# Gate and up projections of a SwiGLU block in seven half-width products per pair of blocks, weight sums on VectorE

## The chip, the cores and the metric

One core of a Trainium2 chip. The metric is the device time of one execution in microseconds (us); the time before is the median of three runs. TensorE (PE) multiplies, PEld is its weight load, VectorE (DVE) and ScalarE (ACT) do elementwise work, GpSimd (POOL) does a little, SyncE (SP) starts the transfers. A "release" below is the moment at which an instruction's input or its buffer becomes available.

## The reference, cut to what matters

Two layers; each is a mixer (a state-space half and a retention half), cross-attention to a memory, and a SwiGLU block. Only the last is changed:

```python
def swiglu(h, w_gate, w_up, w_down):
    return (jax.nn.silu(h @ w_gate) * (h @ w_up)) @ w_down
# h: 512 tokens x 1024, w_gate and w_up: 1024 x 2816, w_down: 2816 x 1024, all f32
x = x + swiglu(rms_norm(x, norm_ffn[l]), w_gate[l], w_up[l], w_down[l])
```

## The kernel before, in words

Everything is transposed: activations lie as 128 channels by 512 tokens, so the hidden width 2816 is 22 blocks f of 128, and the inner width 1024 is 8 blocks kt. Each f32 operand is cut into two parts of the type fp32r, a rounded copy (hi, made by ACT) and the rest (lo, a subtraction on DVE); a product of two such operands is three matmuls, hi*hi, hi*lo and lo*hi (`mm3`, lines 469 to 473). The norm's gain goes into the activations before the product (`Norm.tile`, lines 599 to 608), its 1/rms into the result afterwards (`nrm.bc`).

Weights come in chunks of 128x1024 (512 KB). `prep_chunk` (451 to 459) loads one into a slot of the kind `raw`, and makes hi and lo in two slots of the kind `w`; `chunk` asks for them four chunks ahead in program order. There are 3 raw slots and 6 w slots, that is three chunks of hi and lo. Other tiles of 128x512 come from 66 slots of the kind `u`, and PSUM from 8 banks.

`ffn` (1337 to 1367) runs over parts of the hidden width (`FPARTS`, line 32: three parts in layer 0, four in layer 1). In a part, for each f, `proj` forms gate and up, each as 24 matmuls of 512 columns into one bank; then DVE multiplies both by `nrm.bc`, ACT takes the silu, DVE multiplies the two, and `split` cuts the result into hi and lo. After the part's last f the down projection adds the part's share to x for each of 8 output blocks. In layer 0, four pieces of the next layer's state-space tables (`s5_spill`) are hung behind f = 5, 9, 13 and 17. The last part of layer 1 goes through `last_down`, in two halves of 256 columns.

The program order is not the order on the engines. All operations are recorded, and a planner (`Program.due` and `schedule`, lines 247 to 379) lays them out: it prices each (`price`), gives each a due time from its users, and in a simulated time gives each free engine the most urgent operation whose inputs and slots are ready, TensorE included, which may so take matmuls of a later product first. A slot is handed out when its first operation is placed, and comes back 250 ns after its last reader. `KEEP` is a number of u slots held back from work that is due late.

All instructions are issued through one line of `emit` (387; memsets 385), so the profile gives that line for nearly everything: tiles tell the groups apart. In the names of the profile, `u_nfh` and `u_nfl` are the hi and lo of the SwiGLU's input, `u_gs` and `u_us` gate and up, `u_acth` and `u_actl` the product's parts, `u_xoh` and `u_xol` the input of the cross-attention's output projection (`co`), which runs just before; `u_mh` and `u_ml` are the memory's parts, whose key projection multiplies 256 columns (the memory has 256 rows).

Of the kernel before, what the change touches and what calls it, by code (L numbers as in the profile page):

```python
# [10 lines left out]
F32 = mybir.dt.float32  # L11
F32R = mybir.dt.float32r
I32 = mybir.dt.int32
AF = mybir.ActivationFunctionType
# [4 lines left out]
P = 128  # L19
L = 2  # L20
D = 1024
KT = D // P
SEQ = 512
# [7 lines left out]

FPARTS = (((0, 8), (8, 15), (15, 22)), ((0, 7), (7, 13), (13, 19), (19, 22)))
HALF = SEQ // 2


# [9 lines left out]

KINDS = {"u": 66, "s": 40, "raw": 3, "w": 6, "ps": 8}
LOOKAHEAD = 4
# [9 lines left out]
TABLE, REUSE, COLD, WINDOW = 15000, 250, 7000, 30000  # L57
KEEP, FRONT = {"u": 38}, 30000

# [9 lines left out]
def chunk_order():  # L69

    o = []
    for l in range(L):
        o += [("u", l, m) for m in range(4)]
        o += [("v", l, m) for m in range(4)]
        count = {"q": 1, "k": 1, "g": 1, "ck": KT, "glu": 2, "cv": 8}
        for step in PLAN[l].split():
            key = {"Q": "q", "K": "k", "G": "g", "M": "ck", "L": "glu", "V": "cv"}.get(step[0])
            if key:
                m = int(step[1:] or 0)
                o += [(key, l, m + i) for i in range(count[key])]  # L80
        o += [("out", l, m) for m in range(KT)]
        o += [("cq", l, m) for m in range(KT)]
        o += [("co", l, m) for m in range(KT)]
        for a, b in FPARTS[l]:
            for f in range(a, b):
                o += [("gate", l, f), ("up", l, f)]
            o += [("down", l, f) for f in range(a, b)]
    return o


# [5 lines left out]
class Buf:  # L96
    __slots__ = ("kind", "real", "wr", "rd", "left", "end", "n", "s", "dt")

# [96 lines left out]
class Program:  # L195
    def __init__(self, slots):
        self.ops, self.slots = [], slots
        self.cap = CAP

    def buf(self, kind, s="", dt=None):  # L200
        b = Buf(kind, None, s)
        b.dt = dt
        return Ref(b, (), self.slots[kind][0] if dt is None else self.forms[dt])
# [4 lines left out]
    def add(self, eng, fn, k):  # L208
        o = Op()
# [4 lines left out]
        if fn == "dma_start":  # L214
            o.dur = 60 if eng == "SP" else 1000
            n = 4
            for d in k["out"].ap.shape:
                n *= d
            o.bytes = n
        else:  # L220
            o.dur = price(eng, fn, k)
# [47 lines left out]
    def schedule(self):  # L269
# [7 lines left out]
        self.due()  # L277
        order, left = [], sorted(self.ops, key=lambda o: -o.prio)
        for o in self.ops:
# [4 lines left out]
        def fits(o, low):  # L284
            need = {}
            for b in o.bufs:
                if b.kind and b.real is None:
                    need[b.kind] = need.get(b.kind, 0) + 1
            for k, n in need.items():
                keep = KEEP.get(k, 0) * min(1.0, (o.prio - low) / FRONT)  # L290
                if sum(1 for f, _ in free[k] if f <= t) < n + keep:
                    return False
            return True

        while len(order) < len(self.ops):
            while left and left[-1].end is not None:
                left.pop()
            low = left[-1].prio
            moved = False
            for e in engs:  # L300
# [41 lines left out]
                for b in o.bufs:  # L342
                    if b.kind and b.real is None:
                        f = min(free[b.kind])
                        free[b.kind].remove(f)
                        b.n = f[1]
                        b.real = self.slots[b.kind][b.n] if b.kind != "u" else 0
# [26 lines left out]
            if not nxt:  # L374
                raise RuntimeError(f"no order found: {len(order)} of {len(self.ops)}, next "
                                   f"{left[-1].eng} {left[-1].fn} "
                                   f"{ {k: len(v) for k, v in free.items()} }")
# [22 lines left out]
def trunk(ctx, tc, io):  # L400
# [33 lines left out]
    def gen(s, dt=F32):  # L434
        return prog.buf("u", s, dt)
# [9 lines left out]


    order = chunk_order()
    ready = {}
    state = {"prep": 0, "use": 0}

    def prep_chunk():
        i = state["prep"]
        state["prep"] += 1
        raw = prog.buf("raw")
        Q.dma_start(out=raw, in_=io["w"][i])
        hi, lo = prog.buf("w"), prog.buf("w")
        S.activation(out=hi, in_=raw, func=AF.Copy)
        V.tensor_tensor(out=lo, in0=raw, in1=hi.bitcast(F32), op=sub)
        ready[i] = (hi, lo)

    def chunk(*key):
        i = state["use"]
        state["use"] += 1
        assert order[i] == key, (order[i], key)
        while state["prep"] < min(len(order), i + 1 + LOOKAHEAD):
            prep_chunk()
        return ready.pop(i)

    def mm3(ps, a, b, start, stop):
# [121 lines left out]
    class Norm:  # L591


        def __init__(self, s, gcol, n=SEQ):
            self.s, self.gcol, self.n = s, gcol, n
            self.parts = [None] * KT
            self.acc = None

        def tile(self, i, x, stat=True):
            g = vec[:, self.gcol + i:self.gcol + i + 1]  # L600
            n = self.n
            hi, lo = gen(self.s + "h", F32R), gen(self.s + "l", F32R)
# [733 lines left out]

    def ffn(l, nrm, nxt, extra):
        for fa, fb in FPARTS[l]:
            acts = []
            for f in range(fa, fb):  # L1340
                pg = proj("gate", l, f, nrm)
                if f == 0:
                    nrm.root(True)
                pu = proj("up", l, f, nrm)
                gs, us = gen("gs"), gen("us")
# [5 lines left out]
                if f in extra:  # L1351
                    extra[f]()
            if nxt is None and fb == NFF:
# [142 lines left out]
    for l in range(L):  # L1496
        n_cross = Norm("nc", V_CROSS + l * KT)
        kv = mixer(l, nrm, n_cross, start if l == 0 else lambda: None)
        n_ffn = Norm("nf", V_FFN + l * KT)
        cross(l, n_cross, kv, n_ffn)  # L1500
# [17 lines left out]
def layout(inp):  # L1518
# [11 lines left out]
            "gate": f("w_gate"), "up": f("w_up")}  # L1530
    order = chunk_order()
    w = np.empty((len(order), P, D), np.float32)
    for n, (key, l, m) in enumerate(order):
# [21 lines left out]
    a["w"] = w  # L1555
    cols = lambda k: f(k).reshape(-1, P).T
    a["vec"] = c(np.concatenate(
# [46 lines left out]
```

## Time and profile before

| what | value |
|---|---|
| median of 3 runs | 1525.04 us (1524.87 to 1525.72) |
| the profiled execution | 1526.83 us, of which the span is 1525.1 us |
| mean granted clock of TensorE | 0.990 of 2.4 GHz |
| PE busy | 1499.2 us, 98% |
| DVE busy | 946.9 us, 62% |
| ACT busy | 655.0 us, 43% |
| gate and up of layer 1's second part | 1263.9 to 1329.7 us |
| its down projection | 1329.7 to 1362.7 us |

The shares are means over stages that differ. An instruction's duration on DVE and ACT is longer than the distance at which the next one can start, so costs are read as distances between starts in stretches without a gap, for matmuls too.

### The profile page before, as it was taken

The page shows a single profiled execution, that of the slowest core. Times are in us where ns is not written, and L with a number is a line of the kernel's source. Part 1 is how long each engine was busy: PE and PEld are TensorE (multiplying, and loading weights), DVE is VectorE, ACT ScalarE, POOL GpSimd, SP SyncE. Part 2 cuts the span into 40 slices and gives each one's busy share as a digit, 9 for nine tenths or more (in the row PEclk, how much of TensorE's full clock was granted, in tenths as well). Part 3 has the DMA queues.
Part 4 walks back from the last instruction along what each step waited for, and adds up shares of the span by engine and source line. Part 5 has one row for each costly group of instructions (what it writes and reads, how often), then busy time and mean ns, then how long its engine had stood idle before and what let it go on. Part 6 is the DMA issues. An engine that isn't in the chain of part 4 may idle for free.

```text
span 1525.1 us, 18872 instructions
## 1 busy us (share of the span) xinstructions
PE 1499.2 (98%) x7176; PEld 1241.0 (81%) x7176; DVE 946.9 (62%) x1602; ACT 655.0 (43%) x1050; POOL 90.3 (6%) x192
## 2 busy tenths in 40 slices
PE   8799999999999999999999999999999999999997
PEld 7688888888888888888888879788888888888887
DVE  7899986665674366454554889657656434434445
ACT  5577655444443244243335455544344322323224
POOL 4630000000011010000000000000000000000001
PEclk9899999999999999999999999999999999999998
DMA  6323444321334343344245554433123333333331
GB/s 208 104 85 111 135 120 141 97 70 56 97 114 130 97 140 123 116 125 119 93 132 173 158 165 128 128 104 97 56 70 97 97 97 97 97 97 95 93 94 65
DMA packets 66140, 168.53 MB, mean 111 GB/s; under 512 B 11137, under 2 KB 22785, under 8 KB 66049
## 3 DMA queue, kind: packets, MB, share of 16 engines
q1 hardware_dynamic: 63808, 159.98, 34.7%
q0 software_dynamic: 2240, 7.34, 1.2%
q8 instruction: 56, 0.92, 0.2%
q14 instruction: 36, 0.29, 0.1%
HBM read 152.88 MB, written 13.63 MB: 109 GB/s over the span
## 4 chain that ended last, share of the span: by engine, by line
PE 91%; DVE 4%; POOL 2%; ACT 1%; DMA 1%; issue 1%; SPq 0%; DVEq 0%; ACTq 0%
PE ps L387 91%; DVE w L387 1%; DMA x<-in_xT_dram 1%; POOL s L387 1%; DVE u_gw L387 1%; DVE s L387 0%; POOL u_s5bb L387 0%; DVE u_la L387 0%; SPq L387 0%; ACT u_lq L387 0%; ACT w L387 0%; ACT u_lp L387 0%; DVE u_ly L387 0%; DVE u_gna L387 0%; DVE u_nma L387 0%
## 5 line engine op out<-in xcount | busy, mean ns | idle before, releaser
L387 DVE TENSOR_TENSOR w<-raw,w 128x1024 fp32r<-128x1024 f32 x254 | 310.5, 1226 | 336.5 <-PE ps L387 282.3
L387 ACT ACTIVATE w<-raw 128x1024 fp32r<-128x1024 f32 x254 | 267.6, 1059 | 572.2 <-PE ps L387 502.2
L387 PE MATMUL ps<-u_nfh,w 128*128 128x512 f32 x1408 | 438.7, 391 | 0.0
L387 PEld LDWEIGHTS ps<-u_nfh,w 128*128 128x128 f32 x1408 | 264.4, 188 | 57.3
L387 PE MATMUL ps<-u_nfl,w 128*128 128x512 f32 x704 | 276.9, 393 | 0.0
L387 PE MATMUL ps<-u_acth,w 128*128 128x512 f32 (+1 forms) x752 | 221.5, 377 | 0.0
L387 PEld LDWEIGHTS ps<-u_acth,w 128*128 128x128 f32 x752 | 138.1, 188 | 27.3
L387 PE MATMUL ps<-u_nmh,w 128*128 128x512 f32 x480 | 157.9, 401 | 1.1 <-DVE u_zi L387 1.1
L387 PEld LDWEIGHTS ps<-u_nfl,w 128*128 128x128 f32 x704 | 132.2, 188 | 29.3
L387 PE MATMUL ps<-u_actl,w 128*128 128x512 f32 (+1 forms) x376 | 142.1, 379 | 0.0
L387 PEld LDWEIGHTS ps<-u_nmh,w 128*128 128x128 f32 x480 | 90.3, 190 | 20.0 <-DVE u_zi L387 1.3
L387 PE MATMUL ps<-u_nml,w 128*128 128x512 f32 x240 | 94.9, 396 | 0.0
L387 DVE TENSOR_TENSOR x<-ps,x 128x512 f32<-128x512 f32 x80 | 55.0, 687 | 50.1 <-PE ps L387 50.1
L387 PE MATMUL ps<-u_nch,w 128*128 128x512 f32 x256 | 81.9, 392 | 0.0
L387 PEld LDWEIGHTS ps<-u_actl,w 128*128 128x128 f32 x376 | 70.6, 188 | 13.3
L387 PE MATMUL ps<-u_xoh,w 128*128 128x512 f32 x256 | 80.7, 393 | 0.0
L387 PEld LDWEIGHTS ps<-u_nch,w 128*128 128x128 f32 x256 | 48.0, 188 | 10.5
L387 PEld LDWEIGHTS ps<-u_xoh,w 128*128 128x128 f32 x256 | 48.0, 188 | 9.8
L387 POOL TENSOR_TENSOR u_fin<-u_lp,u_lbc 128x512 f32<-128x512 f32 x4 | 5.6, 1422 | 815.1 <-ACT u_lbc L387 815.1
L387 PEld LDWEIGHTS ps<-u_nml,w 128*128 128x128 f32 x240 | 45.6, 190 | 9.3
L387 ACT ACTIVATE u_acth<-u_us 128x512 fp32r<-128x512 f32 x44 | 27.8, 631 | 56.7 <-DVE u_us L387 56.7
L387 PE MATMUL ps<-u_ncl,w 128*128 128x512 f32 x128 | 50.4, 394 | 0.0
(354 smaller groups left out, 2317.4 us busy)
## 6 DMA issues: line engine op xcount, KB each, us to landing
raw<-in_w_dram SPq DMA_DIRECT2D x254, 512.0 KB, 3.6
u_s5x<-sp SPq DMA_DIRECT2D x28, 256.0 KB, 4.2
u_mr<-in_memT_dram SPq DMA_DIRECT2D x12, 256.0 KB, 4.2
x<-in_xT_dram SPq DMA_DIRECT2D x8, 256.0 KB, 4.5
tu<-u_u SPq DMA_DIRECT2D x8, 256.0 KB, 3.1
u_ub<-tu SPq DMA_DIRECT2D x32, 64.0 KB, 3.9
tu<-u_z SPq DMA_DIRECT2D x8, 256.0 KB, 2.5
u_zt<-tu SPq DMA_DIRECT2D x32, 64.0 KB, 3.6
```

What stands on the lines that cost most here:

```text
L387: getattr(engines[o.eng], o.fn)(**k)
```

## The change

The 2816 columns are taken two blocks f at a time, the inner width two blocks kt at a time (x the even one, y the odd one), and the tokens in two halves of 256. Each such 2x2x2 product takes seven half-width products in place of eight. Four banks X, Y, Z, W hold sums of them; the steps' order and their operands are in `STEPS`. For each pair of blocks, of gate or of up, VectorE makes the four weight sums in place in the two raw slots, between the cuts into hi and lo: wa, wb and wd of 128x1024, wc of 128x512. `forms_of` makes the seven token forms of each pair of input tiles. The banks are read into two tiles as steps end (`keep`), gate and up pairs run as interleaved chains (`run_pairs`), `nrm.bc` enters the gate twice (once for up), and parts of the hidden width become even in size. There are 58 u, 5 raw and 8 w slots, and raw and w slots are handed out strictly in program order (`QUEUED`).

```diff
-FPARTS = (((0, 8), (8, 15), (15, 22)), ((0, 7), (7, 13), (13, 19), (19, 22)))
+FPARTS = (((0, 6), (6, 12), (12, 18), (18, 22)), ((0, 6), (6, 12), (12, 18), (18, 22)))
-KINDS = {"u": 66, "s": 40, "raw": 3, "w": 6, "ps": 8}
+KINDS = {"u": 58, "s": 40, "raw": 5, "w": 8, "ps": 8}
-KEEP, FRONT = {"u": 38}, 30000
+KEEP, FRONT = {"u": 24}, 30000
+QUEUED = ("raw", "w")
...
         def fits(o, low):
+                    if b.kind in QUEUED and b.q != turn[b.kind]:
+                        return False
...
+    def prep_pair(at):
+        i = place[at]
+        h = 512
+        a, b = prog.buf("raw", "pa"), prog.buf("raw", "pb")
+        Q.dma_start(out=a, in_=io["ws"][i, 0])
+        Q.dma_start(out=b, in_=io["ws"][i, 1])
+        V.tensor_tensor(out=b[:, :h], in0=b[:, :h], in1=b[:, h:], op=add)
+        wa = parts_of(a, "wa", 2 * h)
+        wb = parts_of(b, "wb", 2 * h)
+        finish()
+        V.tensor_tensor(out=b[:, :h], in0=b[:, :h], in1=a[:, :h], op=add)
+        V.tensor_tensor(out=a[:, :h], in0=b[:, :h], in1=b[:, h:], op=sub)
+        wc = parts_of(b[:, :h], "wc", h)
+        def last():
+            V.tensor_tensor(out=a[:, h:], in0=a[:, h:], in1=b[:, :h], op=add)
+            ready[at] = (wa, wb, wc, parts_of(a, "wd", 2 * h))
+        held.append(last)
+    def finish():
+        while held:
+            held.pop()()
...
+    STEPS = (("X", 0, 0, "b11"), ("Y", 0, 1, "b21"), ("Z", 1, 0, "t1"), ("W", 1, 1, "t4"),
+             ("X", 2, 0, "t2"), ("Z", 3, 1, "b22"), ("X", 3, 0, "t3"))
+    def pair_steps(key, forms, done):
...
+        for i, (bk, wi, half, form) in enumerate(STEPS):
...
+            for kt in range(n):
+                sl = slice(half * h + kt * P, half * h + kt * P + P)
+                f = forms[kt][form]
+                mmh(ps, ws[wi][0][:, sl], ws[wi][1][:, sl], f, first and kt == 0,
+                    kt == n - 1)
+            done(i, ps)
+            yield
+    def mmh(ps, ah, al, f, start, stop):
+        o = ps[:, :HALF]
+        T.matmul(out=o, lhsT=ah, rhs=f[:, :HALF], start=start, stop=False, ...)
+        T.matmul(out=o, lhsT=ah, rhs=f[:, HALF:], start=False, stop=False, ...)
+        T.matmul(out=o, lhsT=al, rhs=f[:, :HALF], start=False, stop=stop, ...)
+    def run_pairs(gens):
...
+            for k in range(5 if i == 0 else 2):
+                step(g)
+            nx = gens[i + 1] if i + 1 < len(gens) else iter(())
+            for k in range(3):
+                step(nx)
+                step(g)
...
+    def forms_of(x, y, s):
...
+        def form(name, src):
+            f = gen(s + "f", F32R)
+            S.activation(out=f[:, lo], in_=src, func=AF.Copy)
+            V.tensor_tensor(out=f[:, hi], in0=src, in1=f.bitcast(F32)[:, lo], op=sub)
+            out[name] = f
+        form("b11", x[:, lo])
+        form("b21", y[:, lo])
+        V.tensor_tensor(out=t1, in0=x[:, lo], in1=x[:, hi], op=sub)
+        form("t1", t1)
+        V.scalar_tensor_tensor(out=t2, in0=t1, scalar=-1.0, in1=y[:, hi], op0=mul, op1=sub)
+        V.tensor_tensor(out=t4, in0=t2, in1=y[:, lo], op=add)
...
+        V.tensor_tensor(out=t3, in0=y[:, hi], in1=x[:, hi], op=sub)
...
     def ffn(l, nrm, nxt, extra):
+        def keep(x, y):
+            def done(i, ps):
+                o = ps[:, :HALF]
+                if i == 0: S.activation(out=x[:, lo], in_=o, func=AF.Copy)
+                if i == 1: V.tensor_tensor(out=x[:, lo], in0=o, in1=x[:, lo], op=add)
+                if i == 2: S.activation(out=y[:, hi], in_=o, func=AF.Copy, scale=-1.0)
+                if i == 3: S.activation(out=y[:, lo], in_=o, func=AF.Copy)
+                if i == 4: S.activation(out=x[:, hi], in_=o, func=AF.Copy)
+                if i == 5: V.tensor_tensor(out=x[:, hi], in0=o, in1=x[:, hi], op=add)
+                if i == 6: V.scalar_tensor_tensor(out=both(y), in0=wide(ps), scalar=-1.0, ...)
...
-            for f in range(fa, fb):
-                pg = proj("gate", l, f, nrm)
...
-                V.tensor_tensor(out=gs, in0=pg, in1=nrm.bc, op=mul)
-                S.activation(out=gs, in_=gs, func=AF.Silu)
-                V.tensor_tensor(out=us, in0=pu, in1=nrm.bc, op=mul)
-                V.tensor_tensor(out=us, in0=gs, in1=us, op=mul)
-                acts.append(split(us, "act"))
+            for f in range(fa, fb, 2):
...
+                    for g in gs:
+                        V.tensor_tensor(out=g, in0=g, in1=nrm.bc, op=mul)
+                        S.activation(out=g, in_=g, func=AF.Silu)
+                        V.tensor_tensor(out=g, in0=g, in1=nrm.bc, op=mul)
...
+                    for g, u in zip(gs, us):
+                        V.tensor_tensor(out=u, in0=u, in1=g, op=mul)
+                    acts.extend(split(u, "act") for u in us)
...
+            run_pairs(gens)
```

(In `keep` two lines of the source stand on one here.) The weights of a pair lie in a second array, `ws`, laid out on the host; the bytes loaded are the same.

## Rows read from the trace of the kernel before

**Rows 1.** The page, busy time of each engine and its share of the span:
```profile
PE 1499.2 (98%) x7176; PEld 1241.0 (81%) x7176; DVE 946.9 (62%) x1602; ACT 655.0 (43%) x1050; POOL 90.3 (6%) x192
```

**Rows 2.** The page, the chain that ended last, by engine:
```profile
PE 91%; DVE 4%; POOL 2%; ACT 1%; DMA 1%; issue 1%; SPq 0%; DVEq 0%; ACTq 0%
```

**Rows 3.** Busy time by stretch: gate and up, then down, of one part; layer 0's SwiGLU:
```profile
1263.90:1329.70 65.80, 65.80 (x290) 53.97 (x288) 28.84 (x34) 19.69 (x23) 0.00 (x0) 1.00 0.31 96
1329.70:1362.70 33.00, 33.00 (x146) 27.08 (x145) 13.96 (x16) 7.01 (x7) 0.00 (x0) 1.00 0.32 96
...
403.60:766.00 362.40, 362.40 (x1644) 297.06 (x1643) 197.12 (x306) 135.71 (x190) 27.75 (x55) 1.00 0.38 116
```

**Rows 4.** Order in time, PE in gate and up (start, duration), first and last of 12:
```profile
416.88 0.39 PE L387 MATMUL ps<-u_nfl,w 128*128 128x512 f32 x1
...
424.44 0.39 PE L387 MATMUL ps<-u_nfl,w 128*128 128x512 f32 x1
```

**Rows 5.** Order in time, PE in the memory's key projection, first and last of 12:
```profile
182.88 0.28 PE L387 MATMUL ps<-u_ml,w 128*128 128x256 f32 x1
...
186.77 0.28 PE L387 MATMUL ps<-u_ml,w 128*128 128x256 f32 x1
```

**Rows 6.** Order in time, VectorE in the mixer of layer 0, stretches without a gap:
```profile
105.22 0.67 DVE L387 TENSOR_TENSOR u_si<-u_si,u_su 128x512 f32<-128x512 f32 x1
105.83 1.21 DVE L387 TENSOR_TENSOR w<-raw,w 128x1024 fp32r<-128x1024 f32 x1
106.96 0.27 DVE L387 TENSOR_TENSOR u_pa<-ps,tri 128x128 f32<-128x128 f32 x1
...
116.15 0.42 DVE L387 TENSOR_TENSOR u_mt<-u_s5bb,rr 128x256 f32<-128x256 f32 x1
116.48 0.75 DVE L387 TENSOR_TENSOR u_mt<-u_s5bb,ri 128x256 f32<-128x256 f32 x2
...
117.49 0.68 DVE L387 TENSOR_TENSOR u_zu<-ps,u_rs 128x512 f32<-128x512 f32 x1
118.09 0.68 DVE L387 TENSOR_TENSOR u_zt<-ps,u_rs 128x512 f32<-128x512 f32 x1
```

**Rows 7.** Order in time, VectorE, an operation that needs the one before it:
```profile
1160.75 0.69 DVE L387 SCALAR_TENSOR_TENSOR u_nfrt<-u_nfrt,u_nfm 128x512 f32<-128x512 f32 x1
1161.47 0.69 DVE L387 SCALAR_TENSOR_TENSOR u_nfry<-u_nfrt,u_nfry 128x512 f32<-128x512 f32 x1
```

**Rows 8.** Groups of instructions, forms apart (count, busy us, mean ns of one), ACT:
```profile
L387 ACT ACTIVATE w<-raw 128x1024 fp32r<-128x1024 f32 x254 | 267.6, 1059 | 572.2 <-PE ps L387 502.2 <-issue 39.8 <-DMA raw<-in_w_dram 29.9
...
L387 ACT ACTIVATE u_gs<-u_gs 128x512 f32<-128x512 f32 x44 | 27.7, 629 | 18.6 <-DVE u_gs L387 18.5
...
L387 ACT ACTIVATE u_lq<-u_ly 128x256 f32<-128x256 f32 x16 | 6.0, 409 | 3.3 <-DVE u_ly L387 3.3
```

**Rows 9.** Busy time by stretch, the mixer of layer 0 where VectorE is full:
```profile
80.00:180.00 100.00, 99.71 (x527) 81.07 (x527) 96.53 (x214) 74.02 (x128) 12.48 (x13) 1.00 0.35 103
100.00:140.00 40.00, 40.00 (x232) 32.91 (x233) 39.87 (x88) 26.94 (x48) 8.53 (x9) 1.00 0.28 79
```

**Rows 10.** Order in time, a part's last f into its down projection:
```profile
1331.83 0.69 DVE L387 TENSOR_TENSOR u_us<-u_gs,u_us 128x512 f32<-128x512 f32 x1
...
1332.55 0.63 ACT L387 ACTIVATE u_acth<-u_us 128x512 fp32r<-128x512 f32 x1 [1.36 <-DVE u_us L387]
...
1333.21 0.69 DVE L387 TENSOR_TENSOR u_actl<-u_us,u_acth 128x512 fp32r<-128x512 f32 x1 [0.70 <-ACT u_acth L387]
```

**Rows 11.** Waits of PE, the longest for a weight part (total, times, longest):
```profile
PE ps L387 <- DVE w L387: 2.6, 1, 2.6
```

**Rows 12.** Busy time by stretch, around that wait (PEclk is the third number from the end):
```profile
968.00:969.00 1.00, 0.00 (x0) 0.00 (x0) 1.00 (x3) 1.00 (x2) 0.00 (x0) 1.00 0.00 0
969.00:970.00 1.00, 0.00 (x0) 0.00 (x0) 1.00 (x2) 1.00 (x2) 0.00 (x0) 0.99 0.00 0
970.00:971.00 1.00, 0.96 (x2) 0.83 (x3) 1.00 (x2) 0.33 (x1) 0.00 (x0) 0.50 0.00 0
...
973.00:974.00 1.00, 1.00 (x5) 0.77 (x5) 0.46 (x1) 0.04 (x1) 0.00 (x0) 0.80 0.52 131
```

More of the change, by code (lines that the diff above doesn't have):

```diff
@@ L277, in schedule @@
         self.due()
-        order, left = [], sorted(self.ops, key=lambda o: -o.prio)
+        turn = dict.fromkeys(self.slots, 0)
+        order = []
+        left = sorted((o for o in self.ops if o.eng == "PE"), key=lambda o: -o.prio)
+        low = 0.0
         for o in self.ops:
@@ L297, in schedule @@
                 left.pop()
[L298 removed]
+            if left:
+                low = left[-1].prio
             moved = False
@@ L447, in trunk, with prep_chunk @@
     order = chunk_order()
+    place = {}
+    for kind in (3, 5):
+        place.update((i, n) for n, i in enumerate(i for i, x in enumerate(order) if len(x) == kind))
     ready = {}
     state = {"prep": 0, "use": 0}
-    def prep_chunk():
-        i = state["prep"]
-        state["prep"] += 1
+    held = []
+    def prep_chunk(i):
+        finish()
         raw = prog.buf("raw")
-        Q.dma_start(out=raw, in_=io["w"][i])
+        Q.dma_start(out=raw, in_=io["w"][place[i]])
         hi, lo = prog.buf("w"), prog.buf("w")
@@ L464, in chunk @@
         assert order[i] == key, (order[i], key)
-        while state["prep"] < min(len(order), i + 1 + LOOKAHEAD):
-            prep_chunk()
-        return ready.pop(i)
+        ahead, j = 0, i + 1
+        while ahead < max(LOOKAHEAD, 2) and j < len(order):
+            ahead += 2 if len(order[j]) == 5 else 1
+            j += 1
+        while state["prep"] < j:
+            k = state["prep"]
+            state["prep"] += 1
+            (prep_pair if len(order[k]) == 5 else prep_chunk)(k)
+        if i not in ready:
+            finish()
@@ new lines, in finish @@
+    def finish():
[4 more added lines that the diff above has]
+    def pair_steps(key, forms, done):
+        n = len(forms)
+        h = n * P
+        ws = chunk(*key)
+        banks = {}
+        for i, (bk, wi, half, form) in enumerate(STEPS):
+            first = bk not in banks
+            ps = banks.setdefault(bk, None) or bank("p" + bk)
+            banks[bk] = ps
+            for kt in range(n):
[5 more added lines that the diff above has]
+            yield
@@ new lines, in mmh @@
+    def mmh(ps, ah, al, f, start, stop):
+        o = ps[:, :HALF]
+        T.matmul(out=o, lhsT=ah, rhs=f[:, :HALF], start=start, stop=False,
+                 skip_group_check=True)
+        T.matmul(out=o, lhsT=ah, rhs=f[:, HALF:], start=False, stop=False,
+                 skip_group_check=True)
+        T.matmul(out=o, lhsT=al, rhs=f[:, :HALF], start=False, stop=stop,
+                 skip_group_check=True)
+    def run_pairs(gens):
+        gens = list(gens)
+        step = lambda g: next(g, None)
+        for i, g in enumerate(gens):
+            for k in range(5 if i == 0 else 2):
[4 more added lines that the diff above has]
+                step(g)
+            for _ in g:
+                pass
@@ L1555, in layout @@
     a["w"] = w
+    ps = pair_order()
+    ws = np.empty((len(ps), 2, P, D), np.float32)
+    for n, (key, l, fa, fb, m) in enumerate(ps):
+        for r in range(2):
+            blk = f("w_" + key)[l][:, (m + r) * P:(m + r + 1) * P].reshape(-1, 2, P, P)
+            ws[n, r] = blk.transpose(2, 1, 0, 3).reshape(P, D)
+    a["ws"] = ws
     cols = lambda k: f(k).reshape(-1, P).T
```

94 lines of the change are left out of this document (75 added, 19 removed).

## The prediction

> **What bounds the kernel now.** I read the page first: PE is busy for 98% of the span and VectorE for 62% [rows 1]. Then the chain of work that ended last, since a busy PE need not be the bound: 91% of it is PE's [rows 2]. Then the busy time by stretch, because only the SwiGLU blocks change. In gate and up of one part PE has no idle time in 65.8 us, VectorE works 28.84 us of it and ScalarE 19.69; in the part's down projection VectorE works 13.96 of 33.0 us [rows 3]. So here PE sets the time, and VectorE has 56% of gate and up free. Every matmul less is a gain as long as what is added to VectorE fits beside the remaining ones.
>
> **What is removed and added on PE.** Gate and up were 88 blocks (22 of each in two layers) of 24 matmuls of 512 columns, 2112 in all. Twelve third matmuls stand 7.56 us apart from first to last, which is 33 matmuls, so one takes 0.2291 us [rows 4]; 2112 x 0.2291 = 483.8 us. Now there are 44 chains (pairs of blocks of gate or of up), each of 7 steps x 4 pairs of inner blocks x 3 = 84 matmuls of 256 columns, 3696 in all. The memory's key projection has this very form, a weight load before each, hi loaded twice, then lo: 3.89 us for 33, so 0.1179 us each [rows 5]; 3696 x 0.1179 = 435.7 us. A chain takes 9.90 us where it took 10.99. The difference is **-48.1 us**, the most that the change can give.
>
> **What is added on VectorE.** Costs are distances between starts: 0.60 us for 512 elements (0.60 from PSUM also), 1.13 for 1024, 0.33 for 256 [rows 6]; an operation right behind the one that it needs starts 0.12 later, 0.72 [rows 7]. Per chain the weights took two subtractions of 1024, 2.26 us. Now: four sums of 512, 2.40; lo of wa, wb and wd, 3.39; lo of wc, 0.60; together 6.39. Reading the banks adds two sums of 256 and one pass over 512, 1.26. The four passes over gate and the four over up stay eight of 512 for two chains, 2.40 a chain. VectorE's work is 10.05 us a chain against about 4.66 before (the stretch says 28.84 / 6 = 4.81), and PE's is 9.90. So inside gate and up VectorE has become as long as PE. That is the crux.
>
> A part does not have to carry all of it. While the down projection runs, three of the four weight pairs of the first chain can be made (8 w slots are four pairs, one still in use): 0.60 + 2 x 1.13 + 2 x 0.60 + 0.60 = 4.7 us. The last up's merge, 3.0 us, falls into the down projection; its first two chunks must be cut before, 2.3. For six chains: 60.3 - 4.7 - 3.0 + 2.3 = 54.9 us in 59.4 of PE, 92%. The down projections have 33.0 - 14.0 = 19 us free for the rest [rows 3].
>
> Over a whole SwiGLU block the sum is this. Layer 0 had 197.1 us on VectorE in 362.4 [rows 3], its four pieces of state-space tables among it: 22 f x (28.84 + 13.96) / 6 = 157 us are the block itself, so some 40 us are other work. Added are 22 x 5.39 = 119 us and the token forms, per pair of input tiles 7 x 0.33 + 4 x 0.33 = 3.6 against 1.2 before, 10 us for four pairs: 326 us. PE needs 362.4 - 24 = 338. That is 96%. Layer 1 has the same without most of the 40 us: some 290 in 338, 86%. ScalarE is no bound: per chain three copies of 1.06, one of 0.63, four bank reads of 0.41 and two passes of 0.63 make 6.7 us of 9.9 [rows 8].
>
> **What VectorE at its limit costs.** The nearest row is the mixer of layer 0, where VectorE is busy for 96.5 us of 100 and PE for 99.7; in 40 of these, 39.87 and 40.00 [rows 9]. So this planner can keep PE fed by a full VectorE. But there the work lies in many slots; weights here have four pairs, handed out in a fixed order. That order is wa and wb of the next chain, then wd of this one, then wc of the next. Following it, wd gets the pair that wb leaves after step 4, and PE wants it two steps on, 24 x 0.1179 = 2.83 us later; ScalarE's copy and VectorE's subtraction need 1.06 + 1.23 us and handovers of 0.03 [rows 8, 6, 10]. 0.4 us are spare; with another subtraction of 1.13 in front of it wd is 0.7 late. wa has four steps, 5.7 us, wb and wc more. PE may take the next chain's second step meanwhile, which is ready. So a chain loses between 0 and 0.8 us.
>
> The terms: layer 1, 22 chains x 0.25 = 5.5 us (0 to 18). Layer 0, where the other 40 us compete: I take VectorE to reach 93% of the time, below the mixer's 96.5 because of the slots, so 326 / 0.93 = 350, 12 us above PE's 338 (0, if it does as in the mixer, to 24 at 90%). The start of each block: after the last `co` product come the sum into x, the gain, a copy, a subtraction, 0.69 + 0.71 + 0.41 + 0.42 us, and PE has two steps less three matmuls, 2.5 us, without the last odd tile; with the other forms and weight parts queued on the same two engines I take 1.5 us each, 3 in all (0 to 6). The ends of the eight parts: two hidden blocks become ready together instead of one; their path is as in [rows 10], one pass longer, and PE has the other blocks of several outputs to do meanwhile; 2 us (0 to 11, when all 1.4 us are seen). The mixers and the cross-attention lose 8 u slots and get another order: 4 us (0 to 10; a gain is no more than the 2.6 us of the one long wait [rows 11]). The transfers move the same bytes at the same rate, 116 GB/s and less [rows 3], and cost nothing beside five raw slots.
>
> Sum: -48.1 + 5.5 + 12 + 3 + 2 + 4 = -21.6. The profiled execution took 1526.8 us, 1.8 more than the median; 1526.8 - 21.6 - 1.8 = 1503.4, so **about 1503 us**, 1.4% faster.
>
> **Rival 1, PE keeps everything.** All the waits are hidden as in the mixer. For it: [rows 9]. Against it: four weight pairs instead of dozens of slots, and 96% over all of layer 0. Some 5 us are left for starts and mixers: 1525 - 48 + 5 = 1482 us.
>
> **Rival 2, VectorE sets the pace.** In gate and up a chain takes VectorE's 10.05 us, plus dependences (the in-place sums, two of 0.12) and the gaps in which it waits for ScalarE or a slot. For it: 10.05 is above 9.90, and the sums are in a row on the same two slots. At 4% of gaps a chain takes 10.7: 44 x (10.99 - 10.7) = 13 us are gained, and the 9 of starts, ends and mixers go off: some 1521 us, no change. Against it: work can move into the down projections.
>
> **Rival 3, the clock falls: slower.** The one long wait of PE for a weight part, 2.64 us, is followed by three microseconds in which the granted clock is 0.50, the lower of its two levels, 1.2 GHz [rows 11, 12]. Such a wait costs 2.6 us and then 1.6 more, 4.2. If wd is that late in one chain out of four, 11 times, that is 46 us, and the gain is gone: that is the point from which it decides. In every second chain it is 92 us: 1525 - 48 + 92 = 1569. Against it: 2.6 us late means two operations of VectorE ahead of wd and no matmul of the next chain ready, and waits that stay below half a microsecond left the clock at 1.00 in [rows 9]. The Trainium skill, "TensorE: Matmul & The Clock Gate", section "Why this matters for your kernels", asks for no idle gaps above some 3 us between bursts of matmuls. By that rule gaps of about 1 us would cost only themselves, and this case's 2.64 us gap shows that less than its figure can be enough. The skill's "Perfetto Trace Analysis", section "Optimization Strategy", says that the same gap repeated on the engine that should be full can mean that the next tile finds no room in SBUF. By that rule each chain would show the gap at wd, which is the upper bound of 0.8 us a chain above; no trace before the change shows it.
>
> **How the numbers follow.** The forecast with its terms moved inside their bounds (1490 to 1517) gets 0.52, rival 1 (1478 to 1490) 0.13, rival 2 (1517 to 1530) 0.18, rival 3 or another wait as dear 0.17. A measurement of this kernel tells 0.2%, 3 us, from no change. Faster are the forecast, rival 1 and a third of rival 2, 0.71; the same, part of rival 2, 0.07; slower, its rest and rival 3, 0.22. The range leaves out half of rival 1's lower end and the far part of rival 3: 1484 to 1534.
>
> **What the profile after would show.** Matmuls of 256 columns at 0.118 us, 3696 of them; if they are slower, the first term is wrong. VectorE above 90% busy in gate and up, and some 5 us more than now in a down projection of 33. Idle time of PE in front of step 6 of a chain (weights wd), below 1 us at a time, more of it in layer 0. The granted clock 1.00 throughout both blocks; stretches at 0.50 in gate and up mean rival 3. Gate and up of a six-block part in 60 to 62 us against 65.8; 65 means rival 2. A mixer that grows by over 10 us would mean that the slots, not the products, decide.

## The result and the profile after

The changed kernel takes **1488.06 us** (median of 4 runs, 1486.04 to 1489.35) against 1525.28 us (4 runs), a ratio of 0.9755 (95% interval 0.9738 to 0.9772): 37 us faster. The forecast was 1503 us with the range 1484 to 1534, so the sign was right and the time lies in the range. But it lies in the window that the prediction gave to rival 1 (1478 to 1490), outside the forecast's own (1490 to 1517): the waits were put far too high.

The page of the kernel after: busy time by engine, the chain that ended last, and the group of the gate and up matmuls. They answer to [rows 1, 2].

```profile
PE 1453.2 (98%) x8784; PEld 1281.4 (86%) x8784; DVE 1195.7 (80%) x2078; ACT 795.4 (54%) x1372; POOL 95.1 (6%) x192
...
PE 82%; DVE 11%; POOL 2%; issue 2%; ACT 2%; DMA 1%; SPq 0%; DVEq 0%; POOLq 0%; ACTq 0%
...
L403 PE MATMUL ps<-u_nff,w 128*128 128x256 f32 x3696 | 442.6, 280 | 1.8 <-DVE w L403 1.6
```

PE has lost 46.0 us of busy time and is still busy for 98%. VectorE went from 62% to 80% and from 4% to 11% of the chain that ended last. In front of all 3696 new matmuls PE was idle for only 1.8 us (waits in front of other matmuls are not in this row).

Busy time by stretch, after (as [rows 3]: length, then PE, PEld, DVE, ACT, POOL, the granted clock, the DMA share, GB/s). The first two are gate and up, then down, of one six-block part of layer 1; the third is layer 0's SwiGLU from its first gate matmul to the next mixer's first.

```profile
1226.55:1286.40 59.85, 59.55 (x506) 59.21 (x505) 56.56 (x81) 35.84 (x58) 0.00 (x0) 1.00 0.32 110
1286.40:1319.40 33.00, 33.00 (x147) 27.00 (x146) 17.87 (x24) 7.24 (x9) 0.00 (x0) 1.00 0.26 89
...
407.70:762.90 355.20, 350.53 (x2475) 325.07 (x2474) 318.46 (x520) 201.59 (x332) 30.41 (x55) 1.00 0.37 125
```

Gate and up of the part take 59.85 us where they took 65.80 [rows 3], with VectorE 94% busy, and TensorE's own 504 matmuls at 0.1179 us are 59.4 us. The down projection keeps its 33.0 us and now carries 17.87 us of VectorE work in place of 13.96.

The timeline of VectorE (start, duration) through one chain of layer 1, and PE's line of the same time:

```profile
1348.27 0.68 DVE L403 TENSOR_TENSOR w<-raw,w 128x512 fp32r<-128x512 f32 x1
1348.87 0.68 DVE L403 TENSOR_TENSOR raw<-raw,raw 128x512 f32<-128x512 f32 x1
...
1358.36 0.68 DVE L403 TENSOR_TENSOR w<-raw,w 128x512 fp32r<-128x512 f32 x1
...
1339.72 22.44 PE L403 MATMUL ps<-u_nff,w 128*128 128x256 f32 x187
```

The lo of wc comes once in each chain. Here it comes again after 10.09 us, and VectorE has no gap in between: the prediction's 10.05 us a chain, against PE's 9.90, is what happens. Yet PE runs through 22.44 us, more than two chains, without a stop. The question is therefore why an engine that is longer inside the chain does not bind.

Where the time went, from the profiled executions (us). The stages end at the first gate matmul of layer 0, the first matmul of layer 1's mixer, and the last of its cross-attention's output projection:

| kernel | to layer 0's SwiGLU | layer 0's SwiGLU | mixer and cross, layer 1 | layer 1's SwiGLU to the end | median of all runs |
|---|---|---|---|---|---|
| before | 403.8 | 371.5 | 372.6 | 377.2 | 1525.3 |
| after | 407.7 | 355.2 | 369.7 | 353.6 | 1488.1 |
| no weight sums | 408.7 | 348.1 | 369.6 | 350.7 | 1476.9 |
| one pass more | 405.6 | 357.4 | 369.5 | 354.0 | 1489.5 |
| two passes more | 407.3 | 362.9 | 369.6 | 356.4 | 1497.7 |
| planner alone | 406.4 | 371.5 | 369.5 | 376.4 | 1525.3 |
| pieces in the mixer | 406.5 | 341.9 | 378.3 | 354.0 | 1481.4 |
| first piece later | 406.4 | 350.5 | 369.5 | 353.9 | 1481.3 |

Each row is one execution. The first stage, where the kernels with the products hardly differ, goes from 405.6 to 408.7 us here, so a difference of some us there says little; the last stage, in the three of them whose work there is the same (after, pieces in the mixer, first piece later), from 353.6 to 354.0. Half of the 48.1 us, 24.05, was to be had in each block. Layer 1's SwiGLU gave 23.6 of it, layer 0's 16.3. The other two stages together lost 1.0.

### The profile page after: what moved, and what is told of

It reads as the page before. It is cut to its first block, busy times and chain, and to the rows that moved or that the text cites. A ratio compares the mean times of both kernels' runs of the same rounds, so it can differ in the third digit from the quotient of the medians.

```text
span 1486.2 us, 23012 instructions
## 1 busy us (share of the span) xinstructions
PE 1453.2 (98%) x8784; PEld 1281.4 (86%) x8784; DVE 1195.7 (80%) x2078; ACT 795.4 (54%) x1372; POOL 95.1 (6%) x192
## 4 chain that ended last, share of the span: by engine, by line
PE 82%; DVE 11%; POOL 2%; issue 2%; ACT 2%; DMA 1%; SPq 0%; DVEq 0%; POOLq 0%; ACTq 0%
PE ps L403 82%; DVE w L403 3%; DVE raw L403 2%; POOL s L403 1%; DVE u_gs L403 1%; DVE u_us L403 1%; ACT w L403 1%; DVE u_mt L403 0%; DVE u_gw L403 0%; DMA u_w<-in_w_dram 0%; DMA x<-in_xT_dram 0%; SPq L403 0%; DVE u_actl L403 0%; DVE u_la L403 0%; DVE u_rr L403 0%
## 5 line engine op out<-in xcount | busy, mean ns | idle before, releaser
L403 ACT ACTIVATE w<-raw 128x1024 fp32r<-128x1024 f32 (+1 forms) x342 | 342.1, 1002 | 417.0 <-PE ps L403 336.2
L403 PE MATMUL ps<-u_nff,w 128*128 128x256 f32 x3696 | 442.6, 280 | 1.8 <-DVE w L403 1.6
L403 PEld LDWEIGHTS ps<-u_nff,w 128*128 128x128 f32 x3696 | 438.0, 188 | 6.1 <-DVE w L403 3.3
L403 DVE TENSOR_TENSOR w<-raw,w 128x1024 fp32r<-128x1024 f32 (+1 forms) x342 | 391.0, 1150 | 58.2 <-ACT w L403 57.8
L403 DVE TENSOR_TENSOR x<-ps,x 128x512 f32<-128x512 f32 x88 | 60.4, 689 | 100.4 <-PE ps L403 100.2
L403 DVE TENSOR_TENSOR raw<-raw 128x512 f32<-128x512 f32 x88 | 60.5, 687 | 9.6 <-DMA raw<-in_ws_dram 9.3
L403 DVE TENSOR_TENSOR raw<-raw,raw 128x512 f32<-128x512 f32 x88 | 60.1, 683 | 0.4
L403 DVE TENSOR_TENSOR u_gs<-u_gs,u_nfry 128x512 f32<-128x512 f32 x88 | 58.8, 681 | 0.3
L403 PEld LDWEIGHTS ps<-u_nch,w 128*128 128x128 f32 x256 | 48.1, 188 | 10.5
L403 PE MATMUL ps<-u_xol,w 128*128 128x512 f32 x128 | 50.4, 393 | 0.0
```

The source lines that it names most:

```text
L403: getattr(engines[o.eng], o.fn)(**k)
```

## The experiments

### How much VectorE work a chain can bear

Three kernels change only the work on the weight sums: without the four sums of 512 elements, with one more pass over 512 elements in each pair that leaves the values as they are (0.60 us), with two such passes (1.20 us).

```diff
 # no weight sums: the four lines of raw sums are gone
-        V.tensor_tensor(out=b[:, :h], in0=b[:, :h], in1=b[:, h:], op=add)
...
-        V.tensor_tensor(out=b[:, :h], in0=b[:, :h], in1=a[:, :h], op=add)
-        V.tensor_tensor(out=a[:, :h], in0=b[:, :h], in1=b[:, h:], op=sub)
...
-            V.tensor_tensor(out=a[:, h:], in0=a[:, h:], in1=b[:, :h], op=add)
 # one pass more; two passes more have this line twice
+        V.scalar_tensor_tensor(out=b[:, :h], in0=b[:, :h], scalar=0.0, in1=b[:, :h], op0=mul, op1=add)
```

> The four weight sums of each chain are left out (so gate and up come out as other numbers); VectorE does 2.4 us less per chain, PE the same. Theory A (VectorE stands right at its limit: it is 98% busy in a gate-and-up stretch of layer 1 and PE is never idle there): layer 1 gains nothing, since PE is the bound already; layer 0, which is 7.9 us above PE's work, gives back most of that; 1480 to 1484 us. Theory B (VectorE has real room, the 7.9 us of layer 0 are something else): 1486 to 1489 us.

> One more pass of VectorE over 512 elements per chain (0.60 us, b = 0*b + b, the values stay), 26.4 us in all. Theory A: in a stretch of six chains 3.6 us are added and 1.3 are free, so about 2.3 us a part and 8 a layer show in layer 1, more in layer 0; 1504 to 1514 us. Theory B (room of 5% or more, because work moves into the down projections): 1488 to 1493 us.

> Two more such passes per chain, 52.8 us in all. Theory A: nearly all of the second pass shows, 26 us on top of the run with one; 1528 to 1540 us, no better than before the change. Theory B: under 15 us above the change, 1490 to 1503 us.

Measured: 1476.87 us without the sums (ratio 0.9679, 0.9663 to 0.9695), 1489.53 with one pass more (0.9761, 0.9746 to 0.9776), 1497.71 with two (0.9810, 0.9790 to 0.9829). The sums cost 11 us, the next 0.6 us a chain about 1, the next after that about 8. So the cost is neither nothing nor in proportion to the work. Without the sums the time lies below the ranges of both theories: layer 1, which theory A put at nothing, gave back 2.9 us, and layer 0 7.1. The runs with more passes lie in theory B's ranges. How layer 1 takes the work is read from the same part with two passes more, down and then the next part's gate and up:

```profile
1295.10:1328.40 33.30, 33.24 (x146) 26.93 (x145) 23.11 (x32) 7.16 (x9) 0.00 (x0) 1.00 0.28 93
1328.40:1388.30 59.90, 59.90 (x506) 59.33 (x505) 58.06 (x85) 35.94 (x58) 0.00 (x0) 1.00 0.32 108
```

A chain's VectorE work is now 11.25 us against PE's 9.90, 67.5 us for six chains in a stretch of 59.9 us, and still the stretch does not grow. VectorE is at 58.06 there, and the down projection carries 23.11 us of its work in place of 17.87. What counts there is VectorE's sum over gate, up and down. In layer 0's SwiGLU, which has the pieces' work too, that sum rises from 318.46 to 340.72 us, and 7.7 of the 9.6 us that two passes cost in median are lost in this stage; half of that is one stand of TensorE (see the section on the first piece). The theory by which each chain runs at VectorE's pace fell here: it needed some 8 us in layer 1 with the first pass, and the stage lost 0.4.

### The planner, the slots and the parts

Four kernels leave the products alone. "Planner alone" is the kernel before with the changed kernel's slots, queue and planner (a changed price and a few smaller lines of it); "six w" and "parts of eight" change one line of the kernel after; "pieces at the ends" moves the last three of the four pieces of state-space tables.

```diff
 # planner alone (on the kernel before)
-KINDS = {"u": 66, "s": 40, "raw": 3, "w": 6, "ps": 8}
+KINDS = {"u": 58, "s": 40, "raw": 5, "w": 8, "ps": 8}
-KEEP, FRONT = {"u": 38}, 30000
+KEEP, FRONT = {"u": 24}, 30000
+QUEUED = ("raw", "w")
...
-            o.dur = 60 if eng == "SP" else 1000
+            o.dur = 60 if eng == "SP" else 700
...
+                    if b.kind in QUEUED and b.q != turn[b.kind]:
+                        return False
...
 # six w (on the kernel after)
-KINDS = {"u": 58, "s": 40, "raw": 5, "w": 8, "ps": 8}
+KINDS = {"u": 62, "s": 40, "raw": 5, "w": 6, "ps": 8}
 # parts of eight (on the kernel after)
-FPARTS = (((0, 6), (6, 12), (12, 18), (18, 22)), ((0, 6), (6, 12), (12, 18), (18, 22)))
+FPARTS = (((0, 8), (8, 16), (16, 22)), ((0, 8), (8, 16), (16, 22)))
 # pieces at the ends (on the kernel after)
-            extra["work"] = {5 + 4 * c: c for c in range(4)}
+            extra["work"] = {5: 0, 11: 1, 17: 2, 21: 3}
```

> The kernel before with the planner and the slots of after (58 u, 5 raw, 8 w, slots in order, 24 kept), and none of the products. Theory A (slots and planner move the mixers by a few us only, the gain is all of the products): 1523 to 1531 us. Theory B (a part of the 37 us comes from the planner): below 1520 us.

> 6 w slots (three pairs) in place of 8, 62 u slots in place of 58. Theory A (the four pairs are just enough, each chain then waits at a weight part): PE loses 0.5 to 1 us a chain, 20 to 40 us in all, 1508 to 1530 us. Theory B (TensorE takes matmuls of the next chain meanwhile and slots hardly matter): 1486 to 1494 us.

> Parts of 8, 8 and 6 hidden blocks in place of 6, 6, 6 and 4: gate and up stretches of eight chains, and fewer down projections between them. Theory A (VectorE gets its time back in the down projections that follow, so a longer stretch brings it nearer to its limit, 81 us of VectorE in 79): 2 to 4 us a long stretch, 1492 to 1502 us. Theory B (VectorE's limit plays no part): 1484 to 1489 us, since a start and an end of a part fall away in each layer.

> The four pieces of state-space tables of layer 0 are hung behind the last block of each part (f = 5, 11, 17, 21) in place of 5, 9, 13, 17, so that their VectorE work falls due in down projections. Theory A (layer 0 loses 7.9 us against PE's work because the pieces compete with the weights in gate and up, and PE stands behind their small matmuls): the SwiGLU of layer 0 gets 4 to 7 us shorter, 1481 to 1485 us. Theory B (the loss is VectorE's total, 318 of 355 us, wherever the pieces lie): no change, 1486 to 1490 us.

Measured: planner alone 1525.29 us (1.0002, 0.9993 to 1.0012), six w 1491.26 (0.9778, 0.9764 to 0.9793), parts of eight 1491.59 (0.9780, 0.9766 to 0.9795), pieces at the ends 1487.27 (0.9754, 0.9739 to 0.9768). Planner alone lies in theory A's range: the planner and the slots are worth nothing by themselves. The stage before layer 0's SwiGLU takes 2.6 us more and the mixer of layer 1 3.1 us less, as in the kernel after. The whole gain is the products'. Two w slots fewer (with four u slots more) cost layer 1's SwiGLU 1.3 us and layer 0's 3.9 against the kernel after, and the two other stages moved by -8.5 and +5.4 us; the total is in theory B's range, so four pairs of weights are no tight limit. Parts of eight lie between the two ranges, each SwiGLU block 2.4 to 2.6 us longer. The intervals of these two runs touch that of the kernel after: a loss of some 3 us each, at the edge of the noise. Pieces at the ends lie in theory B's range, so the place of the last three pieces does not matter; theory B's reason, VectorE's total wherever the pieces lie, is not shown by it. The place of the first stayed as it was here, and this kernel shows the same wait as the next view, 3.2 us.

### The first piece of the state-space tables

Layer 0's SwiGLU still lost 7.8 of its 24.05 us, and one row stood out among the waits of PE in that stage. PE in order of time, after (in brackets the idle time before and what ended it):

```profile
464.77 1.22 PE L403 MATMUL ps<-u_nff,w 128*128 128x256 f32 x9
469.22 0.27 PE L403 MATMUL ps<-u_ckr,u_br 128*32 128x64 f32 x2 [3.22 <-ACT u_br L403]
469.71 0.61 PE L403 MATMUL ps<-u_nff,w 128*128 128x256 f32 x3 [0.22 <-DVE w L403]
```

VectorE in the same time, first and last of the piece's passes, and the first weight pass behind them:

```profile
462.39 0.42 DVE L403 TENSOR_TENSOR u_s5bb<-u_s5b,fr 128x256 f32<-128x256 f32 x1
...
468.10 0.42 DVE L403 SCALAR_TENSOR_TENSOR u_cki<-u_mt 128x256 f32<-128x256 f32 x1
468.43 1.22 DVE L403 TENSOR_TENSOR w<-raw,w 128x1024 fp32r<-128x1024 f32 x1
```

For 6.04 us VectorE does nothing but the piece's tables, 18 passes of 256 elements in a row. Two things are late behind them: the table that a small matmul of the piece needs, in front of which PE stands in its order, and the next lo part of a weight, whose pass ends at 469.65 and lets the gate and up matmuls go on at 469.71. So the small matmul is not alone to blame. It is the one that the view names, and the weight behind it would have come no sooner.

The stand is dearer than its length. Busy time by stretch around it, after (the granted clock is the third number from the end):

```profile
467.00:468.00 1.00, 0.00 (x0) 0.00 (x0) 1.00 (x4) 0.39 (x1) 0.00 (x0) 1.00 0.00 0
...
470.00:471.00 1.00, 1.00 (x16) 0.87 (x16) 1.00 (x3) 0.78 (x2) 0.00 (x0) 1.00 0.34 78
471.00:472.00 1.00, 1.00 (x8) 0.91 (x7) 1.00 (x3) 0.45 (x1) 0.00 (x0) 0.62 0.99 401
472.00:473.00 1.00, 1.00 (x7) 1.00 (x7) 1.00 (x2) 1.00 (x2) 0.00 (x0) 0.50 0.12 45
473.00:474.00 1.00, 1.00 (x6) 1.00 (x6) 1.00 (x2) 1.00 (x4) 0.00 (x0) 0.50 0.28 57
474.00:476.00 2.00, 2.00 (x17) 2.00 (x16) 2.00 (x4) 2.00 (x4) 0.00 (x0) 0.84 0.87 286
```

The clock is granted in full while PE stands and for some two microseconds of work behind the stand; then it is 0.50, the lower level of 1.2 GHz, for some 3 us. By these rows the lower clock takes 0.38 + 0.50 + 0.50 + 0.32 = 1.7 us of full-speed work, and the idle time 3.2 + 0.2. This is rival 3's mechanism, once, in front of another matmul than rival 3 named. Three kernels test what it costs. "First piece later" moves all four pieces by four blocks; the place of the last three alone was worth nothing in "pieces at the ends".

```diff
 # first piece later (on the kernel after, and the same line on the kernel before)
-            extra["work"] = {5 + 4 * c: c for c in range(4)}
+            extra["work"] = {9: 0, 13: 1, 17: 2, 21: 3}
 # pieces in the mixer (on the kernel after)
...
-            mats[h] = s5_setup(l, h, *kvs["ld"]) if l == 0 else s5_fetch(l, h)
+            if l == 1 and h == 0:
+                kvs["ld"] = s5_load(1)
+            mats[h] = s5_setup(l, h, *kvs["ld"])
...
-            extra["work"] = {5 + 4 * c: c for c in range(4)}
+            extra["work"] = {}
```

> The four pieces of layer 1's tables are begun at f = 9, 13, 17 and 21 in place of 5, 9, 13 and 17. Theory B (one matmul of the first piece, in front of which TensorE stands 3.2 us, and the lower granted clock of some 3 us behind it are the largest single loss of layer 0's SwiGLU): the stand goes away, layer 0's SwiGLU takes 350 to 352 us in place of 355.2, total 1482 to 1485. Theory A (the loss is spread over the chains): the stand moves or goes but layer 0's SwiGLU stays at 354 to 357, total 1486 to 1491.

> Layer 1's state-space tables are no longer made in four pieces beside layer 0's SwiGLU and spilled; they are made at the start of layer 1's mixer, so their VectorE, ScalarE and TensorE work moves from layer 0's SwiGLU into mixer 1. Theory B (what layer 0 still loses, 16.3 us gained of 24.05 possible, is the pieces: their VectorE work of some 40 us and the matmuls of theirs in front of which TensorE stands): layer 0's SwiGLU falls from 355.2 us to 348 to 350, near layer 1's 353.6 less its end, and the weights of one piece at the block's start no longer wait; mixer 1 grows by 0 to 15 us, so the total is 1483 to 1500. Theory A (VectorE's own pace with the weight sums is what layer 0 loses, the pieces do not matter): layer 0's SwiGLU stays at 353 to 356 and only mixer 1 grows, total 1490 to 1503.

> The kernel before, with the four pieces of layer 1's tables begun at f = 9, 13, 17 and 21 in place of 5, 9, 13 and 17; no product is changed. Theory B (the first piece only hurts where the sums have filled VectorE; before, VectorE had room in layer 0's SwiGLU): no change, 1523 to 1528 us, layer 0's SwiGLU 370 to 373. Theory A (the first piece was badly placed by itself, so that the 7 us which the later place gave the changed kernel are not the products' doing): 1517 to 1521 us, layer 0's SwiGLU 364 to 368.

Measured: first piece later on the kernel after 1481.32 us (0.9706, 0.9688 to 0.9724); pieces in the mixer 1481.37 (0.9710, 0.9695 to 0.9725); first piece later on the kernel before 1525.60 (1.0001, 0.9992 to 1.0011). That is theory B in all three; the first two totals lie 1 to 2 us below its ranges, and layer 0's SwiGLU without the pieces, 341.9 us, well below the 348 to 350 expected. Busy time by stretch, 60 us of the kernel after and then, in the second fence, the same 60 us of the kernel with the first piece later, with its layer 0's SwiGLU:

```profile
410.00:440.00 30.00, 29.57 (x252) 28.85 (x251) 29.31 (x48) 18.12 (x34) 1.68 (x4) 1.00 0.30 107
440.00:470.00 30.00, 26.50 (x221) 25.83 (x220) 30.00 (x55) 20.03 (x36) 1.05 (x2) 1.00 0.25 88
```

```profile
410.00:440.00 30.00, 30.00 (x252) 29.66 (x252) 29.20 (x47) 18.41 (x32) 0.53 (x1) 1.00 0.26 90
440.00:470.00 30.00, 29.95 (x239) 28.82 (x238) 30.00 (x46) 19.98 (x33) 0.53 (x1) 1.00 0.40 140
...
406.40:756.90 350.50, 349.39 (x2476) 323.05 (x2475) 316.60 (x519) 200.54 (x333) 30.43 (x57) 1.00 0.37 126
```

From 440 to 470 us VectorE is busy for 30.00 of 30.00 us in both. PE is at 26.50 in one and at 29.95 in the other: a full VectorE does not starve PE, a full VectorE with six microseconds of other work in one piece can. With the first piece later its passes come between weight passes, never more than five in a row; VectorE there, first and last of them and one weight pass between:

```profile
521.29 0.43 DVE L403 TENSOR_TENSOR u_s5bb<-u_s5b,fr 128x256 f32<-128x256 f32 x1
...
532.91 1.23 DVE L403 TENSOR_TENSOR w<-raw,w 128x1024 fp32r<-128x1024 f32 x1
...
539.47 0.43 DVE L403 SCALAR_TENSOR_TENSOR u_cki<-u_mt 128x256 f32<-128x256 f32 x1
```

The row of 18 is not enough by itself: it is there in parts of eight too, where PE had gate and up matmuls ready for most of it, waited 0.9, 0.7 and 0.6 us, and kept the clock at 1.00. With the first piece later, layer 0's SwiGLU takes 350.5 us, 4.7 less, and PE is idle for 1.1 us of it in place of 4.7. Without any piece it takes 341.9 us and the mixer 378.3, 8.8 us more than in the kernel with the first piece later: 341.9 + 8.8 = 350.7 against 350.5, so pieces that are well placed cost layer 0's SwiGLU what they cost the mixer. In the medians the later place is worth 6.7 us; 4.7 us of it are seen in this stage. On the kernel before the same line moves nothing: there PE was busy for all 371.50 us of layer 0's SwiGLU, with the piece at its first place. Without the sums, with the piece at its first place too, the wait is also gone. Layer 0's SwiGLU before and, in the second fence, without the sums:

```profile
403.80:775.30 371.50, 371.50 (x1683) 304.55 (x1682) 202.25 (x312) 139.26 (x195) 27.75 (x55) 1.00 0.38 116
```

```profile
408.70:756.80 348.10, 347.91 (x2476) 323.63 (x2475) 274.31 (x437) 199.01 (x332) 29.59 (x55) 1.00 0.37 127
```

So the collision exists only since the sums have filled VectorE, and more work makes it dearer. With two passes more, layer 0's SwiGLU, PE's wait in front of the same small matmul, and two stretches of 1 us, one in the wait and one behind it, from three views:

```profile
407.30:770.20 362.90, 354.07 (x2475) 327.30 (x2474) 340.72 (x560) 200.42 (x332) 34.24 (x55) 0.99 0.36 122
...
PE ps L403 <- ACT u_br L403: 5.3, 1, 5.3
...
470.00:471.00 1.00, 0.00 (x0) 0.00 (x0) 1.00 (x4) 0.01 (x1) 0.00 (x0) 0.50 0.00 0
...
478.00:479.00 1.00, 1.00 (x6) 1.00 (x6) 1.00 (x2) 1.00 (x2) 0.00 (x0) 0.50 0.77 217
```

The wait is 3.2 us in the kernel after, 4.4 with one pass more and 5.3 with two, and by the stretches around it the lower clock takes 1.7, 2.8 and 3.5 us of full-speed work. Together that is 4.9, 7.2 and 8.8 us. So all of the 2.2 us that one pass more costs this stage, and 3.9 of the 7.7 us of two passes, are this one stand. Of the other 3.8 us, 1.9 are waits for weight parts (1.3 us in the kernel after, 3.2 with two passes more); the rest was not separated.

### The order of the gate and up matmuls

The prediction let the next chain's ready matmuls cover for a late wd. In this kernel the planner must lay the gate and up matmuls out in strict program order. That order itself puts the first steps of the next chain between the last ones of this chain (`run_pairs`), so only the planner's freedom beyond it is tested.

```diff
+        o.g = None
+        if eng == "PE" and k.get("rhs") is not None and k["rhs"].buf.s == "nff":
+            o.g = self.made.get("gate", 0)
+            self.made["gate"] = o.g + 1
...
+            if o.g is not None and o.g != turn.get("gate", 0):
+                return False
...
+                if o.g is not None:
+                    turn["gate"] = o.g + 1
```

> Only the planner is changed: the 3696 gate and up matmuls must be laid out on TensorE in strict program order (down products and other matmuls stay free to go between). Theory B (a late wd costs little because TensorE takes matmuls of another step or of the next chain meanwhile): each chain loses 0.3 to 0.8 us, 1500 to 1523 us in all, seen as idle time of TensorE in front of wd. Theory A (weights are in time by themselves, the order of the gate and up matmuls hides nothing): 1485 to 1493 us, no more idle time of TensorE than in the changed kernel.

Measured: 1491.41 us (0.9772, 0.9754 to 0.9790), whose interval touches that of the kernel after. Waits of PE for weight parts (total, times, longest), first the kernel after, then this one:

```profile
PE ps L403 <- DVE w L403: 2.3, 5, 0.7
```

```profile
PE ps L411 <- DVE w L411: 3.8, 5, 1.1
```

The total is in theory A's range, though PE waits 1.5 us more for weights than in the kernel after. The freedom of order is worth some 3 us, near the noise, not the 12 to 35 us that a late wd in every chain would give. The weights come nearly in time by themselves.

### One sum on GpSimd

```diff
-        V.tensor_tensor(out=b[:, :h], in0=b[:, :h], in1=b[:, h:], op=add)
+        G.tensor_tensor(out=b[:, :h], in0=b[:, :h], in1=b[:, h:], op=add)
```

> The first of the four sums goes to GpSimd (1.4 us there by the row of u_fin), VectorE does 0.6 us less per chain. Theory A: nothing in layer 1, up to 3 us in layer 0; 1484 to 1488 us. A rival: GpSimd's pass is slower and comes first in a chain, so weights are late, or it slows VectorE's own passes: above 1492 us.

Measured, the rival: 1503.95 us (0.9856, 0.9841 to 0.9871), 16 us slower than the kernel after, 7.9 of it in layer 0's SwiGLU and 9.5 in layer 1's. PE's waits for weight parts in this kernel:

```profile
PE ps L403 <- DVE w L403: 18.2, 23, 1.5
```

The group of these sums on GpSimd, and VectorE's weight passes of 1024 in this kernel (count, busy us, mean ns of one):

```profile
L403 POOL TENSOR_TENSOR raw<-raw 128x512 f32<-128x512 f32 x44 | 69.9, 1588 | 1131.4 <-DMA raw<-in_ws_dram 979.0 <-DVE u_nfa L403 39.2 <-DVE u_actl L403 28.6
...
L403 DVE TENSOR_TENSOR w<-raw,w 128x1024 fp32r<-128x1024 f32 x298 | 374.9, 1264 | 71.9 <-ACT w L403 70.5 <-issue 0.9
```

VectorE in order of time in the same kernel, two weight passes with no sum on GpSimd beside them and two beside the one that GpSimd starts at 631.94 us:

```profile
1195.77 2.36 DVE L403 TENSOR_TENSOR w<-raw,w 128x1024 fp32r<-128x1024 f32 x2
...
631.54 3.92 DVE L403 TENSOR_TENSOR w<-raw,w 128x1024 fp32r<-128x1024 f32 x2 [0.17 <-ACT w L403]
```

VectorE was relieved of 44 x 0.60 = 26 us, and yet it is busy for 320.36 and 287.10 us in the two SwiGLU blocks, against 318.46 and 287.25: its other passes grew by what the sums had taken, 13 us of it in the 298 weight passes of 1024 (1219 ns each in the kernel after, 1264 here). And PE waits 23 times for a weight in place of 5. The sum takes 1.30 us in the median (the mean of 1.59 has one of 6.12 in it) in place of 0.69 and is the first link before ScalarE's copy; what share of the loss this longer path has was not separated.

## Why the prediction was right in sign and off in size

**PE's columns, −48.1.** Right. 22.44 us for the 187 matmuls that the trace holds are 0.120 us each, the few missing records included, against 0.1179, and layer 1's SwiGLU gave 23.6 of the 24.05 us that this term promised for it.

**VectorE's work.** Right: 10.09 us a chain for 10.05; 56.56 us of a six-chain part for 54.9; a down projection up by 3.9 us for 5; in layer 0 116.2 us more in the SwiGLU stage (318.46 against 202.25) and 10.1 more in the stage before it, 126 for the 129 that were to be added. ScalarE, 35.84 of 59.85 us, was no bound.

**Layer 1, a quarter of a microsecond a chain, +5.5, with its share of starts and ends some 8 in all.** This step failed. The loss is 0.5 us, net of what the kernel before lost there itself. The working took wd to be up to 0.7 us late by the order in which four weight pairs are handed out. The waits for weights are 2.3 us in the whole kernel, 0.3 of them in layer 1's SwiGLU; three pairs in place of four cost that stage 1.3 us, and strict order costs the kernel some 3 us. The planner uses the slack of the down projection, and two passes more show how much there is: 1.2 us a chain cost layer 1's SwiGLU 2.8 us. Why wd is in time in each chain was not followed in the trace.

**Layer 0, +12 by a limit of 93% for VectorE.** Over-sized, and for another reason than the one given: the stage lost 7.8 us with its starts and ends, of which 4.7 are the first piece's, and these go away with VectorE as full as before (316.60 of 350.50 us, 90%). The other 3 remain. Without the sums the stage takes 348.1 us, so these are mostly the sums' doing. Whether there is a limit such as 93% stays open: with two passes more VectorE is at 340.72 of 362.9 us, 94%, and the stage loses 7.7 us more, but 3.9 of them are the first piece's stand.

**Starts and ends of the parts, +5; mixers, +4.** Starts and ends are inside the two losses above. The two other stages lost 3.9 and gained 2.9, 1.0 together; the planner alone does about the same to them (2.6 and 3.1) without a product changed.

The sum as measured, with the profiled executions: −48.1 + 7.8 + 0.5 + 1.0 = −38.8, and the profiled executions stand at 1526.83 and 1487.98 us, −38.85.

**The rivals.** Rival 1 is nearest: 1482 us was its figure, and with the first piece later the kernel takes 1481.3. It got 0.13; its evidence [rows 9], a VectorE full for 40 us beside a PE without idle time, deserved more than the worry about slots. Rival 2 needs a part of 65 us and 59.85 was measured. Rival 3 happened once, for some 5 us, and not at wd: its price was of the right size (3.2 us idle, then 1.7 us of lower clock, against 2.6 and 1.6 in [rows 11, 12]), its frequency was not. The sign "granted clock 1.00 throughout both blocks" failed with it. The Trainium skill, "TensorE: Matmul & The Clock Gate", section "Why this matters for your kernels", wants no idle gaps above some 3 us between bursts of matmuls; this stand of 3.2 us agrees, and [rows 12] showed the same behind 2.6 already. The Trainium skill, "Perfetto Trace Analysis", section "Optimization Strategy", says that a gap which repeats on the engine that should be full can mean too little room for the next tile. No gap repeated here: five waits for weights in 44 chains.

## What to carry to other kernels

An engine that is longer than TensorE inside a loop body is no bound as long as its work can be done ahead in a neighbouring stage: compare the sums over the whole stretch in which work can move, not those of the loop body (here a VectorE at 90% of that stretch was nearly free once the first piece was moved). When a change fills an engine, look for what else is on it in one uninterrupted piece; work that was free before, six microseconds in a row here, can take 5 to 7 us from the gain, and moving its start by four blocks gives them back. To price a filled engine, add a pass and then another, and look in each stage for what the added time is: here half of what looked like the engine's limit was one stand that had grown.

## What the runs showed of the hardware

A sum of 512 f32 elements takes GpSimd 1.30 us in the median, against 0.69 us on VectorE, and two VectorE weight passes beside it took 3.92 us in place of 2.36: work moved to GpSimd did not make VectorE's busy time less. After the stand of 3.2 us TensorE's clock did not fall at once: it was 1.00 in the idle time and for some two microseconds of work, and 0.50 only then. In the stands of 4.4 and 5.3 us it fell to 0.50 before the work began again, and stayed there for some 6 and 7 us of work (windows of 1 us around 468 and 473 us of the kernels with one and two passes more).
